# Low parts of the second MLP matrix: an accumulating DMA in place of a subtraction on DVE

## The chip, the cores and the metric

The kernel runs on one core of one Trainium2 chip. The metric is the device time of one execution in microseconds (us); lower is better. TensorE is written PE here, VectorE DVE, ScalarE ACT, GpSimd POOL and SyncE SP, as the profile writes them.

## What is computed

The reference is a decoder trunk of two layers on one sequence of 256 tokens, 1024 channels wide, all in float32. Layer 0 mixes tokens by stick-breaking attention, layer 1 by causal softmax attention with rotary positions (its block selection is void at 256 tokens, since there is one block). After each mixer comes an MLP with a squared ReLU. Cut to what matters here:

```python
def squared_relu_mlp(x, w1, w2):
    return jnp.square(jax.nn.relu(x @ w1)) @ w2
...
    for i in range(DEPTH):
        ln1_g, ln1_b, w1, w2, ln2_g, ln2_b = channel[i]
        h = layer_norm(DEEPNORM_ALPHA * h + mixers[i % N_MIXERS](h), ln1_g, ln1_b)
        h = layer_norm(DEEPNORM_ALPHA * h + squared_relu_mlp(h, w1, w2), ln2_g, ln2_b)
```

`w1` is 1024 x 4096 and `w2` is 4096 x 1024, so each of them is 16 MB per layer.

## The kernel before

**Three products for one.** PE multiplies in the type fp32r. To keep float32 accuracy, every operand is split in two fp32r numbers: `hi`, the operand rounded to fp32r, and `lo`, what the rounding left. Each dense product is then three matmuls, hi by hi, hi by lo and lo by hi (`mm3`, and the three `mm` calls in `projT`), all summed in PSUM. So every weight that comes from memory has to be split on the chip before PE can use it.

**Units.** The weights come in units of 1 MB, tiles of 128 x 4 x 512 float32: for each layer 12 units of `wqkv`, 4 of `wo`, 16 of `w1` and 16 of `w2`, in the order of the list `units`. The units are numbered through both layers, 0 to 95; layer 0 has units 0 to 47. `Unit` queues for each unit one load on SP's DMA queue into a `raw` tile (line 242), and two halves of 128 x 1024, each split by `split`: ACT copies `raw` to `hi`, which rounds (line 203), and DVE subtracts `hi` from `raw` to give `lo` (line 204). There are three `raw` buffers (`RAWS`) and five pairs of `hi` and `lo` (`LIVE`). A `raw` buffer is free again when the second half has been split, a `hi`/`lo` pair when PE has done its last matmul with the unit (`retire`).

**The MLP.** It runs in 8 steps of 512 hidden channels, numbered 0 to 7. `up_tok` (steps 0 and 1) and `up` (steps 2 to 7) multiply by two units of `w1`; ACT and DVE make the squared ReLU (lines 624 and 626), and the hidden values are split as well. `down` multiplies the hidden values of one step by two units of `w2`, first for the first 128 tokens, then for the other 128, and adds all 8 steps up in four PSUM banks. After the two first `up` steps the kernel goes on with up 2, down 0, up 3, down 1 and so on until up 7, down 5; then come down 6 and down 7 and the closing norm. So in steady state one MLP step takes four units from memory: two of `w1` and two of `w2`. In `down` the loop goes over four k with the two units in turn, so the second half of a unit is first needed at k = 2.

**The order of the work.** No scheduler of a library decides it: the class `Plan` does, while the program is built. Each operation is queued with the engine, a cost, the results it needs, the buffer slots it takes and gives back, and a rank; `Plan` keeps a clock for each engine and emits operations in the order in which they can start by these clocks, the most urgent first among those that can start within 0.25 us. PE's dense products stand in the order of the program, and small products slip in between. Once emitted, each engine takes its instructions strictly in that order and waits on semaphores for what they need.

**POOL** has little to do: it fills constants, writes one column in the scores of layer 0, adds the rotary parts in layer 1 (line 540) and takes one power for each norm (line 362).

Of the kernel before, what the change touches and what calls it, by code (L numbers as in the profile page):

```python
# [7 lines left out]
F32 = mybir.dt.float32  # L8
# [3 lines left out]
ALU = mybir.AluOpType  # L12
# [18 lines left out]
MARGIN, WINDOW = 0.5, 0.25  # L31
# [8 lines left out]


class Tok:
    """When the result of one queued operation is there, by the plan's clock (None: not yet emitted)."""

    def __init__(self, eng=None, end=None, lat=0.0):
        self.eng, self.end, self.lat = eng, end, lat
# [3 lines left out]


class Late:
    """Both halves of v, which are queued later than their readers."""

    def __init__(self):
        self.toks = []
# [4 lines left out]


class Plan:
    """Emits the operations of all engines in the order in which they can start.

    TensorE follows the dense products as the program gives them. Everything else is queued with
    its cost (us), the results it needs, the buffer slots it takes and gives back, and a rank
    (lower is more urgent), and is emitted once TensorE's clock has passed its start. Operations
    queued for TensorE itself slip in between the dense products when their operands have been
    there for MARGIN; among operations that can start within WINDOW the most urgent goes first.  # L70
    """

    LAT = {"pe": 0.2, "act": 0.1, "dve": 0.1, "pool": 0.2, "sp": 1.0}

    def __init__(self, slots):
        self.clock = {e: 0.0 for e in self.LAT}
# [77 lines left out]
def trunk(ctx: ExitStack, tc: tile.TileContext, x, xt, cst, cstb, w, ln, out):  # L154
    nc = tc.nc
# [4 lines left out]
    one = pool("one", 1)  # L160
# [9 lines left out]
    plan = Plan({"raw": RAWS, "split": LIVE, "t2k": N2K, "t1k": N1K, "pt": NPT, "kd": NKD, "st": 3, "acc": 4, "wk": 4})  # L170
    clock = plan.clock
# [10 lines left out]
    def act(n, fn, **kw):  # L182
        return plan.op("act", 0.06 + 0.00083 * n, fn, **kw)
# [14 lines left out]
        return Tok("pe", clock["pe"], 0.2)  # L198

    def split(n, hi, lo, src, after, rank=1, take=(), give=(), scale=None):  # L200
        """hi(), lo(), src() give the operands when the operation is emitted."""
        if scale is None:
            f = lambda: nc.scalar.copy(hi(), src())  # L203
            g = lambda: nc.vector.tensor_tensor(lo(), src(), hi().bitcast(F32), op=ALU.subtract)  # L204
        else:
            f = lambda: nc.scalar.mul(hi(), src(), scale)
            g = lambda: nc.vector.scalar_tensor_tensor(lo(), src(), scale, hi().bitcast(F32), op0=ALU.mult, op1=ALU.subtract)
        a = act(n, f, after=after, rank=rank, take=take)
        b = dve(n, g, after=[a], rank=rank, give=give)
        b.first = a  # L210
        return b
# [4 lines left out]
    v = [one.tile([P, D], F32, tag=f"v{t}", name=f"v{t}") for t in range(NT)]  # L216
# [13 lines left out]
    taken = [0]  # L230
    U = []

    class Unit:
        def __init__(self, i):
            name, j = units[i]
            steps = [(k, k + 1) for k in range(4)] if i < 2 else [(0, 2), (2, 4)]
            self.tok = []
            for k0, k1 in steps if i < 2 else [(0, 4)]:
                def load(k0=k0, k1=k1):
                    if k0 == 0:  # L240
                        self.raw = raws.tile([P, 4, 512], F32, tag="raw", name=f"raw{i}")
                    nc.sync.dma_start(self.raw[:, k0:k1, :], w[name][j][:, k0:k1, :])
                ld = plan.op("sp", 0.73 * (k1 - k0), load, rank=3 + 0.01 * i + 0.001 * k0, take=[("raw", 1)] if k0 == 0 else ())
                for c0, c1 in steps:
                    if not (k0 <= c0 and c1 <= k1):
                        continue

                    def hi(c0=c0, c1=c1):
                        if c0 == 0 and not hasattr(self, "hi"):
                            self.hi = splits.tile([P, 4, 512], F32R, tag="hi", name=f"hi{i}")  # L250
                            self.lo = splits.tile([P, 4, 512], F32R, tag="lo", name=f"lo{i}")
                        return self.hi[:, c0:c1, :]
                    b = split(512 * (c1 - c0), hi, lambda c0=c0, c1=c1: self.lo[:, c0:c1, :],
                              lambda c0=c0, c1=c1: self.raw[:, c0:c1, :], after=[ld] + [k.first for k in self.tok[:1]],
                              rank=lambda c0=c0: (0.5 if i < taken[0] else 1 if i < taken[0] + 1 else 2) + 0.001 * i + 0.0001 * c0,
                              take=[("split", 1)] if c0 == 0 else (), give=[("raw", 1)] if c1 == 4 else ())
                    self.tok += [b] * (c1 - c0)

    def take(n):
        i = taken[0]  # L260
# [39 lines left out]
    for k in range(KT):  # L300
        src = xs[k // 4][:, k % 4, :]
        if k in X_LOADS:
            ks = slice(k, k + X_LOADS[k])
            ld = plan.op("sp", max(0.45, 0.365 * X_LOADS[k]), lambda ks=ks: nc.sync.dma_start(
                xs[ks.start // 4][:, ks.start % 4:(ks.stop - 1) % 4 + 1, :], xt[:, ks, :]), rank=3 + 0.01 * (k // 4) + 0.001 * (k % 4) - 0.0005)
        if k == 0:
            hi = dve(T * 0.5, lambda k=k, src=src: nc.vector.tensor_copy(xh[:, k, :], src), after=[ld], rank=0.01 * k)
        else:
            hi = act(T, lambda k=k, src=src: nc.scalar.copy(xh[:, k, :], src), after=[ld], rank=0.5 + 0.00005 * k)
# [92 lines left out]
    for l in range(DEPTH):  # L402
# [2 lines left out]
        mixed = {}  # L405

        def attend(g, pr, src, ready, give):
            """Heads 4g + 2pr and the next: scores, weights, their transposes, the products with v."""
            box = {}

            def part(s, k):
                """s: high or low parts; k: of which head's keys (None: of the queries)"""
                def go():
                    if k is None:
                        box["q"] = box.get("q") or buf("q", F32R)
                        return box["q"][:, s * T:(s + 1) * T]
                    if "kd" not in box:
                        box["kd"] = kd_free.pop(0)
                    return kd[box["kd"]][s][k * HD:(k + 1) * HD, k, :]
                return go  # L420
            ks = []
            for k in (0, 1):
                ks.append(split(T, part(0, k), part(1, k), lambda k=k: src()[k * HD:(k + 1) * HD, T:2 * T],
                                after=ready + [y.first for y in ks], rank=0.9, take=[("kd", 1)] if k == 0 else ()))
            q = split(T, part(0, None), part(1, None), lambda: src()[:, 0:T], after=ready + [y.first for y in ks], rank=0.9,
                      take=[("t2k", 1, 4)], give=give, scale=SCALE)
            s1, p1 = weights(1, box, ks + [q])
            _, p0 = weights(0, box, ks + [q, s1])
            flipped = [flip(j, box, [p1, p0]) for j in range(2)]

            def mix():
                if g // 2 not in OT:
                    OT[g // 2] = (st.tile([P, 4, T], F32R, tag="sh", name="oh"), st.tile([P, 4, T], F32R, tag="sl", name="ol"))
                o = box["o"] = wbank("o")
                for kt in range(2):
                    for j in range(2):
                        hd = 4 * g + 2 * pr + j
                        pt = box["pt", j]
                        nc.tensor.matmul(o[HD * j:HD * j + HD, kt * P:T], v[kt][:, hd * HD:(hd + 1) * HD],  # L439
                                         pt[:, 0:T] if kt == 0 else pt[:, T:T + P], start=kt == 0, stop=kt == 1)  # L440
            m = plan.op("pe", 0.74, mix, after=flipped + [vtok[g // 2]], rank=0.5,
                        take=[("wk", 1)] + ([("st", 1)] if g % 2 == 0 and pr == 0 else []), give=[("pt", 2)])
            pi = 2 * (g % 2) + pr
            mixed[g, pr] = split(T, lambda: OT[g // 2][0][:, pi, :], lambda: OT[g // 2][1][:, pi, :],
                                 lambda: box["o"][:, :T], after=[m], rank=0.8, give=[("wk", 1)])

        def weights(t, box, ready):
            """Scores of two heads for query tile t (head by head along the free axis) and what becomes of them."""
            nk = (t + 1) * P
            n = 2 * nk  # L450
            tag = "t2k" if t else "t1k"

            def scores():
# [6 lines left out]
                if t == 0:  # L460
                    kd_free.append(box["kd"])
            s = plan.op("pe", 0.76 if t else 0.43, scores, after=ready, rank=1.05 - 0.05 * t, take=[("wk", 1, 1)],
                        give=() if t else [("t2k", 1), ("kd", 1)])
            sc = lambda: box["sc", t][:, :n]
            new = lambda name: (t2k if t else t1k).tile([P, 516 if t else 260], F32, tag=tag, name=name)
            if l == 0:
# [7 lines left out]
                k = act(n, sig("keep", -1.0), after=[s], rank=0.7, take=[(tag, 1, 1)])  # L474
                b = act(n, sig("p", 1.0), after=[k], rank=0.69, take=[(tag, 1)], give=[("wk", 1)])
# [312 lines left out]
```

## Time and profile before

| what | us |
|---|---|
| median of 2 runs | 617.45 |
| the two runs | 616.89 and 618.01 |
| span of the profiled execution, first to last instruction | 616.2 |
| PE busy in it | 601.4 |
| DVE busy | 400.9 |
| ACT busy | 300.3 |
| POOL busy | 26.4 |

The profiled execution is told by its span alone; the runs are timed as a whole, so the median stands 1.25 us above the span. An engine's busy time is the time in which at least one of its instructions ran. Matmuls overlap each other in the records (each is shown for longer than the distance to the next), so how fast PE really goes is read from the distance between the starts of two matmuls. A DMA is issued by an engine in a moment and runs on 16 DMA engines that all queues share; "DMA share" is the mean busy share of these 16.

### The profile page before, as it was taken

To read this page: it belongs to the slowest core of one execution; us is meant where nothing else is said; L and a number is where in the kernel's file an instruction comes from. 1 tells how busy PE (TensorE), PEld (TensorE's weight loads), DVE (VectorE), ACT (ScalarE), POOL (GpSimd) and SP (SyncE) were. 2 spreads that over 40 slices of the span, in tenths; PEclk is the share of its full clock that TensorE was granted. 3 is DMA by queue.
4 is the path that set the end of the run, shared out by engine and by line. 5 is a ranking of instruction groups with operands and counts; after the bars stand their busy time and mean duration, and the time that the engine had idled before them with its cause. 6 is when DMAs were issued, how large, how long until landed. Compare 5 with 4: busy or idle time off the path is not lost.

```text
span 616.2 us, 8736 instructions
## 1 busy us (share of the span) xinstructions
PE 601.4 (98%) x3544; PEld 515.7 (84%) x3544; DVE 400.9 (65%) x537; ACT 300.3 (49%) x483; POOL 26.4 (4%) x46
## 2 busy tenths in 40 slices
PE   8999999999999999999999999999999999999994
PEld 6888887888998898898887777778898998898883
DVE  5888776596636446455788868858676536446444
ACT  5866764245535344353436755635365335344310
POOL 2000000000000000000032011101000000000000
PEclk9999999999999999999999999999999999999998
DMA  8875235265564555546273543332874464555201
GB/s 282 348 298 215 82 128 194 76 227 217 200 246 145 202 200 187 199 160 228 71 252 132 189 153 137 138 137 70 271 260 152 169 241 152 198 198 190 84 1 68
DMA packets 17752, 109.32 MB, mean 177 GB/s; under 512 B 1968, under 2 KB 2352, under 8 KB 5680
## 3 DMA queue, kind: packets, MB, share of 16 engines
q1 hardware_dynamic: 17712, 108.76, 48.1%
q8 instruction: 28, 0.46, 0.3%
q14 instruction: 12, 0.10, 0.0%
HBM read 107.71 MB, written 1.05 MB: 176 GB/s over the span
## 4 chain that ended last, share of the span: by engine, by line
PE 87%; DVE 8%; ACT 1%; DMA 1%; issue 1%; POOL 0%; SPq 0%; DVEq 0%; ACTq 0%
PE up_ps L189 29%; PE dn_ps L189 29%; PE wo_ps L189 7%; PE qk_ps L189 5%; PE qkT_ps L189 5%; PE v_ps L189 4%; PE sc L189 2%; DVE lo L204 2%; PE o L439 2%; DVE keep L476 1%; DVE p L479 1%; DMA raw<-in_wqkv 1%; PE xt L378 1%; PE pt_ps L504 1%; PE ht_ps L658 1%
## 5 line engine op out<-in xcount | busy, mean ns | idle before, releaser
L204 DVE TENSOR_TENSOR lo<-raw,hi 128x1024 fp32r<-128x1024 f32 (+1 forms) x196 | 229.7, 1215 | 73.5 <-ACT hi L203 73.0
L203 ACT CAST hi<-raw 128x1024 fp32r<-128x1024 f32 (+1 forms) x196 | 192.2, 1034 | 91.0 <-issue 65.2
L189 PE MATMUL up_ps<-xh,hi 128*128 128x256 f32 x384 | 108.1, 281 | 0.0
L189 PE MATMUL up_ps<-xl,hi 128*128 128x256 f32 x384 | 107.9, 281 | 0.0
L189 PE MATMUL up_ps<-xh,lo 128*128 128x256 f32 x384 | 107.9, 281 | 0.0
L189 PE MATMUL dn_ps<-hi,hl 128*128 128x512 f32 x256 | 100.8, 394 | 0.0
L189 PE MATMUL dn_ps<-lo,hh 128*128 128x512 f32 x256 | 100.2, 392 | 0.0
L189 PE MATMUL dn_ps<-hi,hh 128*128 128x512 f32 x256 | 99.6, 389 | 0.0
L189 PEld LDWEIGHTS up_ps<-xl,hi 128*128 128x128 f32 x384 | 72.3, 188 | 0.5
L189 PEld LDWEIGHTS up_ps<-xh,hi 128*128 128x128 f32 x384 | 72.3, 188 | 0.5
L189 PEld LDWEIGHTS up_ps<-xh,lo 128*128 128x128 f32 x384 | 72.4, 188 | 0.0
L626 DVE SCALAR_TENSOR_TENSOR r<-up_ps,r 128x512 f32<-128x512 f32 x32 | 22.1, 691 | 59.9 <-ACT r L624 59.9
L624 ACT ACTIVATE r<-up_ps 128x512 f32<-128x512 f32 x32 | 19.2, 599 | 77.9 <-PE up_ps L189 77.9
L189 PEld LDWEIGHTS dn_ps<-lo,hh 128*128 128x128 f32 x256 | 48.0, 188 | 10.6
L189 PEld LDWEIGHTS dn_ps<-hi,hh 128*128 128x128 f32 x256 | 48.1, 188 | 10.1
L189 PEld LDWEIGHTS dn_ps<-hi,hl 128*128 128x128 f32 x256 | 48.1, 188 | 9.8
L189 PE MATMUL qkT_ps<-xh,hi 128*128 128x256 f32 x128 | 37.7, 295 | 1.3 <-ACT hi L203 1.3
L189 PE MATMUL qkT_ps<-xh,lo 128*128 128x256 f32 x128 | 36.4, 285 | 0.2 <-DVE lo L204 0.2
L189 PE MATMUL qkT_ps<-xl,hi 128*128 128x256 f32 x128 | 36.3, 283 | 0.0
L203 ACT CAST xh<-xt 128x512 fp32r<-128x512 f32 x12 | 6.7, 589 | 42.9 <-PE xt L378 42.9
L189 PE MATMUL v_ps<-hi,xh 128*128 128x512 f32 x64 | 27.3, 427 | 0.0
L189 PEld LDWEIGHTS qkT_ps<-xh,hi 128*128 128x128 f32 x128 | 24.6, 192 | 2.8 <-ACT hi L203 2.4
(114 smaller groups left out, 922.5 us busy)
## 6 DMA issues: line engine op xcount, KB each, us to landing
raw<-in_w SPq DMA_DIRECT2D x64, 1024.0 KB, 4.8
raw<-in_wqkv SPq DMA_DIRECT2D x22, 1024.0 KB, 5.2
raw<-in_wo SPq DMA_DIRECT2D x8, 1024.0 KB, 4.8
raw<-in_wqkv SPq DMA_DIRECT2D x8, 256.0 KB, 6.3
gb<-in_l_ln_g SPq DMA_DIRECT2D x4, 512.0 KB, 3.8
gb<-in_l_ln_b SPq DMA_DIRECT2D x4, 512.0 KB, 5.3
h<-in_x SPq DMA_DIRECT2D x2, 512.0 KB, 6.1
out<-h SPq DMA_DIRECT2D x4, 256.0 KB, 2.1
```

The source lines that it names most:

```text
L189: nc.tensor.matmul(ps, sta, mov, start=start, stop=stop)
L203: f = lambda: nc.scalar.copy(hi(), src())
L204: g = lambda: nc.vector.tensor_tensor(lo(), src(), hi().bitcast(F32), op=ALU.subtract)
L378: nc.tensor.transpose(ps[:, k * P:(k + 1) * P], h[t][:, (4 * n + k) * P:(4 * n + k + 1) * P], ident)
L439: nc.tensor.matmul(o[HD * j:HD * j + HD, kt * P:T], v[kt][:, hd * HD:(hd + 1) * HD], pt[:, 0:T] if kt == 0 else pt[:, T:T + P], start=kt = ...
L476: c = dve(n, lambda: nc.vector.tensor_tensor_scan(box["keep", t][:, 0:n][:, ::-1], box["keep", t][:, 0:n][:, ::-1], ind[n][:, ::-1], 1.0, ...
L479: return s, dve(n, lambda: nc.vector.tensor_tensor(box["p", t][:, :n], box["p", t][:, :n], box["keep", t][:, 1:n + 1], op=ALU.mult), after ...
L504: nc.tensor.transpose(ps[:, 0:P], p0[:, j * P:(j + 1) * P], ident)
L624: nc.scalar.activation(box["r", n], ps, AF.Relu)
L626: return dve(512, lambda: nc.vector.scalar_tensor_tensor(box["r", n], ps, 0.0, box["r", n], op0=ALU.max, op1=ALU.mult), after=[a], rank=0. ...
L658: nc.tensor.transpose(box["ht"][:, k * P:(k + 1) * P], box["r", 0][:, k * P:(k + 1) * P], ident)
```

## The change

For the units of `w2` of steps 0 to 5 (`j < 12`, 12 of 16 units in each layer, 24 in all) the low part is made in another way. ACT makes `hi` as before. Then ACT writes minus `raw` into the `lo` tile, which rounds it, so that the tile holds minus `hi`. Then POOL issues a DMA that adds `raw` to what stands in the `lo` tile, and leaves raw minus hi there. The DVE subtraction of these units is gone. `raw` is given back when the DMA's second half is done, by the plan's clock of a new queue `gd` with a cost of 0.0016 us per column and a latency of 2.5 us. The comments that the full diff takes out change nothing and are left out here; the lines below line 61 move down by some 20 lines.

```diff
-    LAT = {"pe": 0.2, "act": 0.1, "dve": 0.1, "pool": 0.2, "sp": 1.0}
+    LAT = {"pe": 0.2, "act": 0.1, "dve": 0.1, "pool": 0.2, "sp": 1.0, "gd": 2.5}
...
+                    if by_dma(name, j):
+                        b = self.split_dma(i, c0, c1, hi, ld)
+                        self.tok += [b] * (c1 - c0)
+                        continue
                     b = split(512 * (c1 - c0), hi, lambda c0=c0, c1=c1: self.lo[:, c0:c1, :],
...
+        def split_dma(self, i, c0, c1, hi, ld):
+
+            n = 512 * (c1 - c0)
+            rank = lambda: (0.5 if i < taken[0] else 1 if i < taken[0] + 1 else 2) + 0.001 * i + 0.0001 * c0
+            raw = lambda: self.raw[:, c0:c1, :]
+            lo = lambda: self.lo[:, c0:c1, :]
+            a = act(n, lambda: nc.scalar.copy(hi(), raw()), after=[ld] + [k.first for k in self.tok[:1]], rank=rank,
+                    take=[("split", 1)] if c0 == 0 else ())
+            m = act(n, lambda: nc.scalar.mul(lo(), raw(), -1.0), after=[a], rank=rank)
+            b = plan.op("gd", 0.0016 * n, lambda: nc.gpsimd.dma_start(lo().bitcast(F32), raw(), accum_op=ALU.add), after=[m], rank=rank,
+                        give=[("raw", 1)] if c1 == 4 else ())
+            b.first = m
+            return b
+
+    def by_dma(name, j):
+        return name[:2] == "w2" and j < 12
```

Since `Plan` sets the order of every engine, the change moves instructions. The first place is ACT in a step in the middle of the first MLP, from the squared ReLU of up 4 to that of up 5; units 33 and 36 are of `w1`, 34 and 35 of `w2`, and `up_ps`, `r`, `hh` are the hidden values of the `up` step. Before:

```order
L624 ACTIVATE r_2062<-up_ps_1939 128x512
L203 CAST hi33_2067<-raw33_1933 128x1024
L203 CAST hh_2055<-r_2062 128x512
L203 CAST hi33_2067<-raw33_1933 128x1024
L203 CAST hi34_2084<-raw34_2000 128x1024 x2
L203 CAST hi35_2133<-raw35_2029 128x1024 x2
L203 CAST hi36_2156<-raw36_2106 128x1024 x2
L624 ACTIVATE r_2242<-up_ps_2128 128x512
```

And with the change:

```order
L203 CAST hi33_2079<-raw33_1946 128x1024
L203 CAST hh_2065<-r_2074 128x512
L203 CAST hi33_2079<-raw33_1946 128x1024
L269 CAST hi34_2096<-raw34_2033 128x1024
L271 ACTIVATE lo34_2097<-raw34_2033 128x1024
L269 CAST hi34_2096<-raw34_2033 128x1024
L271 ACTIVATE lo34_2097<-raw34_2033 128x1024
L269 CAST hi35_2147<-raw35_2069 128x1024
L271 ACTIVATE lo35_2148<-raw35_2069 128x1024
L269 CAST hi35_2147<-raw35_2069 128x1024
L271 ACTIVATE lo35_2148<-raw35_2069 128x1024
L203 CAST hi36_2187<-raw36_2119 128x1024 x2
```

Each half of units 34 and 35 now has two instructions on ACT, the copy and the negated copy, one right behind the other; the units keep their order.

On POOL nothing stood between the power of the first norm of a layer and that of its closing norm; now the layer's 24 DMAs stand there, two for each of its 12 units, in the order in which ACT feeds them.

The second place is SP's queue of weight loads in the same steps, with the semaphores that each load waits for. `DVE_49` stands for a DVE instruction, `DMAHW` for an earlier load, `DMASW` for one of POOL's DMAs. Before:

```order
L242 DMA raw37_2123<-in_w10 128x2048 [waits DMAHW5_49,DVE_49]
L242 DMA raw38_2190<-in_w20 128x2048 [waits DMAHW6_49,DVE_49]
L242 DMA raw39_2219<-in_w20 128x2048 [waits DMAHW7_49,DVE_49]
L242 DMA raw40_2296<-in_w10 128x2048 [waits DMAHW0_49,DVE_49]
L242 DMA raw41_2313<-in_w10 128x2048 [waits DMAHW1_49,DVE_49]
```

And with the change:

```order
L242 DMA raw37_2140<-in_w10 128x2048 [waits DMASW5_49,DMAHW5_49,DMASW4_49,Activation_49]
L242 DMA raw38_2227<-in_w20 128x2048 [waits DMAHW7_49,DVE_49]
L242 DMA raw39_2263<-in_w20 128x2048 [waits DMAHW6_49,DMASW7_49,DMASW6_49]
L242 DMA raw40_2313<-in_w10 128x2048 [waits DMAHW0_49,DVE_49]
L242 DMA raw41_2334<-in_w10 128x2048 [waits DMASW1_49,DMAHW1_49,DMASW0_49,Activation_49]
```

The loads stand in the same order. Every second one now waits for two of POOL's DMAs, those of the unit of `w2` whose `raw` buffer it takes over (raw37 that of unit 34, raw39 that of unit 35, raw41 that of unit 38). On PE the dense products keep their order; in each MLP the four small transposes of the second `up_tok` for the second 128 tokens (line 658, `ht_ps`) stand one product of three matmuls earlier.

## Rows read from the trace of the kernel before

**Rows 1.** The page: span; busy time and share of each engine.

```profile
span 616.2 us, 8736 instructions
...
PE 601.4 (98%) x3544; PEld 515.7 (84%) x3544; DVE 400.9 (65%) x537; ACT 300.3 (49%) x483; POOL 26.4 (4%) x46
```

**Rows 2.** Stretches: columns named in the first row.

```profile
core 0: us, PE busy (x) PEld busy (x) DVE busy (x) ACT busy (x) POOL busy (x), PEclk, DMA share, GB/s
...
11.00:28.00 17.00, 16.88 (x112) 15.05 (x113) 14.27 (x23) 14.08 (x29) 0.00 (x0) 1.00 0.90 355
28.00:103.00 75.00, 71.90 (x519) 62.11 (x519) 56.30 (x75) 48.87 (x91) 0.77 (x11) 1.00 0.52 191
103.00:308.00 205.00, 205.00 (x1197) 180.42 (x1194) 125.61 (x145) 91.49 (x114) 2.98 (x3) 1.00 0.49 182
...
404.00:606.00 202.00, 202.00 (x1182) 177.80 (x1179) 118.03 (x137) 82.79 (x103) 2.77 (x3) 1.00 0.45 164
606.00:616.20 10.20, 1.94 (x9) 1.26 (x7) 5.04 (x9) 0.00 (x0) 0.92 (x1) 0.75 0.14 51
```

**Rows 3.** Stretches: one MLP step, columns as in rows 2.

```profile
195.30:217.70 22.40, 22.40 (x146) 20.39 (x146) 11.94 (x12) 10.07 (x13) 0.00 (x0) 1.00 0.50 189
```

**Rows 4.** Groups by line: count, busy us, mean ns, idle before.

```profile
L204 DVE TENSOR_TENSOR lo<-raw,hi 128x1024 fp32r<-128x1024 f32 x188 | 224.2, 1237 | 71.7 <-ACT hi L203 71.2
L203 ACT CAST hi<-raw 128x1024 fp32r<-128x1024 f32 x188 | 187.2, 1052 | 88.0 <-issue 65.2 <-PE qk_ps L189 11.8 <-DMA raw<-in_wqkv 5.1
...
L624 ACT ACTIVATE r<-up_ps 128x512 f32<-128x512 f32 x32 | 19.2, 599 | 77.9 <-PE up_ps L189 77.9
```

**Rows 5.** Timeline of ACT there: start, duration, instruction, idle time before.

```profile
208.86 2.95 ACT L203 CAST hi<-raw 128x1024 fp32r<-128x1024 f32 x3
217.25 3.89 ACT L203 CAST hi<-raw 128x1024 fp32r<-128x1024 f32 x4 [5.45 <-issue]
226.42 0.60 ACT L624 ACTIVATE r<-up_ps 128x512 f32<-128x512 f32 x1 [5.27 <-PE up_ps L189]
...
229.75 1.04 ACT L203 CAST hi<-raw 128x1024 fp32r<-128x1024 f32 x1
```

**Rows 6.** Timeline of DVE in that step.

```profile
218.33 4.63 DVE L204 TENSOR_TENSOR lo<-raw,hi 128x1024 fp32r<-128x1024 f32 x4 [4.63 <-ACT hi L203]
...
230.82 1.22 DVE L204 TENSOR_TENSOR lo<-raw,hi 128x1024 fp32r<-128x1024 f32 x1 [0.25 <-ACT hi L203]
```

**Rows 7.** Timeline of PE there: down ends, later the next begins.

```profile
217.23 0.39 PE L189 MATMUL dn_ps<-lo,hh 128*128 128x512 f32 x1
217.46 0.39 PE L189 MATMUL dn_ps<-hi,hl 128*128 128x512 f32 x1
...
229.28 0.39 PE L189 MATMUL dn_ps<-lo,hh 128*128 128x512 f32 x1
...
229.97 0.39 PE L189 MATMUL dn_ps<-lo,hh 128*128 128x512 f32 x1
...
232.71 0.39 PE L189 MATMUL dn_ps<-lo,hh 128*128 128x512 f32 x1
```

**Rows 8.** Timeline, start of the first MLP: ACT, then PE.

```profile
150.41 0.60 ACT L624 ACTIVATE r<-up_ps 128x512 f32<-128x512 f32 x1 [1.18 <-PE up_ps L189]
...
153.69 0.59 ACT L203 CAST hh<-ht_ps 128x512 fp32r<-128x512 f32 x1 [0.79 <-PE ht_ps L658]
...
162.93 0.39 PE L189 MATMUL dn_ps<-lo,hh 128*128 128x512 f32 x1
```

**Rows 9.** The page: DMA issues, KB each, median us to landing.

```profile
raw<-in_w SPq DMA_DIRECT2D x64, 1024.0 KB, 4.8
...
gb<-in_l_ln_g SPq DMA_DIRECT2D x4, 512.0 KB, 3.8
...
h<-in_x SPq DMA_DIRECT2D x2, 512.0 KB, 6.1
```

**Rows 10.** Line 242, the weight loads: time from issue to landing.

```profile
DMA to landing us min/median/max: 3.0/4.9/9.5
```

## The prediction

> **What bounds the kernel now.** I read the page first, then the kernel cut into stretches, then one MLP step in the timelines. The page says that PE is busy for 601.4 of 616.2 us [rows 1]. The stretches say where the rest lies: from 103 to 308 us and from 404 to 606 us, which hold both MLPs, PE is busy for 205.00 of 205.00 and 202.00 of 202.00 us; the last 10.2 us lack 8.3, the first attention lacks 3.1 [rows 2]. All that the change touches lies in the two stretches without a gap. Busy time alone does not tell that PE goes at its full pace, so I compare distances: with DVE idle two matmuls of a down step start 0.23 us apart (217.23 to 217.46; DVE had been idle for 4.63 us up to 218.33), and with DVE at work 12 of them take 2.74 us (229.97 to 232.71), again 0.23 each [rows 6, 7]. DVE's work does not slow PE, and in an MLP step DVE is busy for 11.94 of 22.4 us, ACT for 10.07, POOL for nothing, the DMA engines for half the time [rows 3]. So PE bounds the MLP, and what is taken from DVE there is taken from an engine that nobody waits for. The question is only whether the new way is late.
>
> **The change, part by part.**
>
> DVE loses 48 subtractions of 1.237 us [rows 4], 59.4 us; in a step 4 of them, so that 11.94 falls to 7.0 us. PE never waits there: worth 0.
>
> ACT gains 48 negated copies. The trace has no such instruction; half its size takes 0.60 us, the plain copy of its size 1.05 [rows 4], so between 1.05 and twice 0.60. I take 1.05: 50 us in all, 4.2 in a step, so 10.07 becomes 14.3 of 22.4. They fit: the copies that began at 208.86 ended at 211.8 and are now done at 213.9, before the next that PE lets go at 217.25; these ended at 221.1, now 223.2, and the squared ReLU that waits behind them came at 226.42 [rows 5]. Worth 0; its cover is 3.2 us, and what is over that would delay hidden values that PE needs over a step later.
>
> POOL gains 48 DMA issues where it did nothing [rows 3]. Behind them on POOL stands only the power of the closing norm, after two more down steps on PE.
>
> Now the wait that takes DVE's place: PE waits for the accumulating DMA. Call A its time from issue to landing. ACT begins unit 35 at 217.25, when PE has let a hi/lo pair go; copy and negated copy of its first half are done 2 x 1.05 later, at 219.35, and PE first reads this low part at 229.97 (the second lo matmul of the step; the first, at 229.28, is unit 34's) [rows 5, 7]. So A may be 10.6 us. The second half is issued at 221.45 and read 12 matmuls later, at 232.71: 11.3 us. Unit 34 is made a down step earlier, from about 209.9 on, and has over 17. The tightest is unit 23, in the first down step of each layer: ACT's ReLU ends at 151.0, three instructions of 1.05 (the last negated copy of unit 22, copy and negated copy of unit 23) stand before the DMA, which is issued at 154.2, and PE reads at 162.93 [rows 8]: 8.8 us.
>
> No DMA of POOL and none that accumulates is in this trace, so A is bounded by the loads: the fastest took 3.0 us, the slowest 9.5 [rows 10]; 512 KB, the size of one half, took 3.8 in one kind and 6.1 in another [rows 9]. I take 4.8, between the last two and what 1 MB takes. Then 4.0 us are spare at unit 23 and 5.8 at unit 35 and its like, and the wait is worth 0. At 9.5, unit 23 comes 0.7 us late, once per layer: +1.4 us. At 3.0 nothing is won, because PE has no gap there to lose.
>
> The `raw` buffer is held until the second DMA has landed, so every second load starts later. Unit 37's load waits for unit 34's second half, which ACT feeds at 213.9: landing at 218.7, the load then lands 4.8 later, at 223.5, and ACT copies unit 37 from 229.75 on [rows 5, 9]. 6.2 us are spare (A up to 11.0). Unit 39's load waits for unit 35: 221.45 + 4.8 + 4.8 = 231.1, and its copy comes a step after 217.25, at 239.6. Worth 0. The loads behind them on SP's queue move with them and have as much.
>
> The DMA engines take on 24 MB more. In a step four loads keep them at 0.50 of 22.4 us [rows 3], 11.2 us, 2.8 for each MB. One accumulating DMA takes 1.4 us of them by the bytes that it writes, 2.8 if its two streams are read one after the other, 4.2 if reading both and writing all add up. I take 2.0, nearer to what 512 KB take now. Four of them make 8.0, together 19.2 of 22.4, a share of 0.86; the engines did 0.90 from 11 to 28 us [rows 2]. Worth 0, with little to spare.
>
> On this price a page of the Trainium skill speaks against the change. "Collectives: The Full Stack", in its section on the bandwidth ceiling, says that an add in the DMA engines costs nothing for the adding, but half the speed, since two sources are read through one ring. By that rule the price is the 2.8 of above and the sum is that of the first rival below; no run here shows it yet.
>
> Last, four transposes in each MLP come three matmuls (0.36 us) earlier on PE; ACT's part of their operand ended at 151.0 and DVE's behind it takes under 1 us, while the copy that waited for them began at 153.69 [rows 8]. Worth 0.
>
> The sum is 0: the span stays 616.2 us, and with the 1.25 us by which the median of the runs stands above it the kernel takes 617.45, so 617.5. By the bounds of A and of the negated copy alone it is 617.4 to 619. A measurement can tell about 2% from no change, 12.3 us.
>
> **The rivals.**
>
> *The DMA engines become the bound.* At 2.8 us a step needs 11.2 + 11.2 = 22.4 us of them. If they do no better than the 0.90 of the fullest stretch [rows 2], a step takes 24.9, 2.5 more. There are six such steps in a layer, 15.0 us; the 5.8 us that unit 35 has to spare are used up first; 9.2 are left, 18.4 in both layers: 636. It passes 12.3 us from 2.7 us per DMA on. At 4.2 a step takes 31.1, and both layers lose 93: 710. For it speaks that the loads alone fill half the time; against it, that a copy of this size now takes half as much.
>
> *The DMA is slow to land.* POOL may need long to issue, or the second half waits behind the first. Since ACT starts unit 35 only when PE gives a pair back, every us of A above 10.6 is lost anew in each step. With A at 12.2, twice the 6.1 us of the slower 512 KB load [rows 9], five units lose 1.6 and unit 23 loses 3.4: 11.4 per layer, 22.8 in both: 640. It passes 12.3 us from A = 11.3 on. Against it: the slowest of all loads, of twice the size, took 9.5 [rows 10].
>
> *PE gains after all.* Then it has to be in its gaps: 14.8 us in all, less the 8.3 at the end that the norm holds [rows 2], leaves 6.5: 611. For it speaks only that DVE is at 65% [rows 1]. Over 2% faster would need nearly all gaps of the kernel.
>
> That the subtraction stays where it was is not open: the instructions are gone from DVE's queue.
>
> **How the numbers follow.** The forecast has 0.70, engines full 0.13, slow landing 0.12, a gain 0.05. Of the two slow cases (0.25) about 0.03 stay under 12.3 us; of the gain 0.02 would have to come from somewhere I don't see. So faster 0.02, same 0.70 + 0.03 + 0.03 = 0.76, slower 0.22. The forecast's own range is 616 to 619. The whole one goes down to 614, half of the possible gain, and up to 640, the price of slow landing, past the 636 of two reads; the three-pass price and slower landings stay outside, about 0.12.
>
> **What would show it.** Right: PE still busy all through both MLPs, DVE busy down by about 59 us and ACT's up by about 50, POOL's DMAs landing within 3 to 9 us, DMA share in a step near 0.86, and the step still 22.4 us from one unit of that kind to the next. Engines full: a share of 0.9 or more through the steps, loads that take 8 us and more, ACT waiting for `raw` and PE for `lo` or `hi` late in each MLP, steps that grow. Slow landing: a wait of PE for the DMA once in every step, always at the second triple of the down step, with a share well below 0.9. The forecast is wrong if PE has any gap of over 1 us in the steps.

## The result, and the profile after

| what | before | after |
|---|---|---|
| median of 2 runs, us | 617.45 | 626.73 (625.18 and 628.29) |
| ratio | | 1.0133, 95% interval 1.0088 to 1.0178 |
| span of the profiled execution, us | 616.2 | 623.4 |

The kernel is 1.3% slower. That is within 2%, as forecast, and inside the whole range of 614 to 640, but outside the forecast's own range of 616 to 619 and 9.2 us above its 617.5. The first experiment below, a longer series of the same kernel, agrees. The profiled execution is the one of 625.18 us, and its span is 7.2 us longer than before; this 7.2 is what the traces can explain.

Line numbers up to 252 are the same in both kernels, those further down are 21 higher with the change (624 becomes 645); L269, L271 and L272 are the copy, the negated copy and the DMA of `split_dma`. The page of after, against [rows 1, 9]; the lines with `q` give packets, MB and the share of all 16 DMA engines over the span:

```profile
span 623.4 us, 8882 instructions
...
PE 603.8 (97%) x3544; PEld 515.0 (83%) x3544; DVE 346.6 (56%) x489; ACT 347.1 (56%) x531; POOL 68.6 (11%) x94
...
q1 hardware_dynamic: 17712, 108.76, 47.3%
q0 software_dynamic: 6912, 25.17, 21.2%
...
raw<-in_w SPq DMA_DIRECT2D x64, 1024.0 KB, 6.9
lo<-raw POOLq DMA_DIRECT2D x48, 512.0 KB, 8.4
```

DVE fell by 54.3 us and ACT rose by 46.8, much as forecast. `q0` is POOL's queue: its 48 DMAs take 21.2% of 623.4 us, 132 us, 2.75 us of all 16 engines each. They land 8.4 us after their issue, and a weight load now takes 6.9 us instead of 4.8.

The stretches of after, against [rows 2, 3]:

```profile
103.00:308.00 205.00, 203.25 (x1186) 177.82 (x1183) 95.81 (x117) 112.27 (x135) 24.08 (x27) 1.00 0.80 241
404.00:606.00 202.00, 198.25 (x1174) 172.96 (x1173) 88.44 (x106) 108.89 (x131) 22.61 (x26) 1.00 0.76 224
150.00:174.50 24.50, 23.26 (x151) 20.88 (x150) 8.78 (x10) 16.52 (x21) 4.50 (x6) 1.00 0.95 278
195.30:217.70 22.40, 22.40 (x146) 20.41 (x145) 7.40 (x8) 13.60 (x17) 3.17 (x5) 1.00 0.96 278
219.20:242.20 23.00, 22.59 (x145) 20.19 (x144) 7.40 (x8) 13.03 (x16) 3.29 (x4) 1.00 0.95 270
```

PE, gapless in both long stretches before, now lacks 1.75 and 3.75 us there. The loss is not spread over the steps: one step (195.30 to 217.70) is as gapless as before and another (219.20 to 242.20) lacks 0.41 us, while the DMA engines are at 0.95 or 0.96 in the three short stretches; in the step from 195.30 to 217.70 they were at 0.50 before. The granted clock of PE is 1.00 in all these stretches, so it has no part in this.

Who waited for a DMA in after (us in total, times, longest):

```profile
ACT hi L203 <- DMA raw<-in_w: 63.9, 14, 7.2
...
PEld dn_ps L189 <- DMA lo<-raw: 9.1, 10, 2.2
...
PE dn_ps L189 <- DMA lo<-raw: 5.4, 6, 1.8
```

And SP's queue of weight loads:

```profile
SPq L242 <- DMA lo<-raw: 179.8, 24, 11.6
```

24 loads now stand until an accumulating DMA has given back their `raw` buffer. That a load waits is not new: in the trace of before SP's queue stood for 468.6 us until DVE's subtractions had given buffers back.

Every wait that PE has in the two long stretches is for the accumulating DMA. Its longest, in the second MLP, in the timeline of PE, with the wait in brackets:

```profile
579.98 0.39 PE L189 MATMUL dn_ps<-hi,hh 128*128 128x512 f32 x1
582.18 0.50 PE L189 MATMUL dn_ps<-lo,hh 128*128 128x512 f32 x1 [1.81 <-DMA lo<-raw]
582.52 0.40 PE L189 MATMUL dn_ps<-hi,hl 128*128 128x512 f32 x1
```

The place is the second low-part matmul of a down step, unit 91's, the kind that [rows 7] priced. From 579.98 to 582.18 it is 2.20 us instead of 0.23, and the next distance is 0.34: 2.08 lost where the bracket shows 1.81. If each of the six waits hides the same 0.27 (an estimate from this one), 5.4 becomes 7.0 of the 7.2 us. So nearly the whole loss of this execution is PE waiting for `lo`. Four of the six waits are for the second half of the step's second unit, two, as here, for its first half.

How a DMA comes to be late, here the second half of the same unit 91, is in the chain of waits of after, cut to 554 to 586 us (start, duration, what):

```profile
554.54 9.18 DMA raw<-in_w
...
563.80 1.05 ACT hi L203
...
573.02 0.96 ACT lo L271
573.99 0.34 issue
574.33 11.61 DMA lo<-raw
...
585.98 4.17 PE dn_ps L189 x17
```

And ACT's row for the copy in it, in the timeline:

```profile
563.80 1.05 ACT L203 CAST hi<-raw 128x1024 fp32r<-128x1024 f32 x1 [6.08 <-DMA raw<-in_w]
```

Read from the top. At 554.54 a weight load starts, that of unit 89, as soon as unit 86's `raw` buffer, which an accumulating DMA had held, is free. It needs 9.18 us. ACT stands idle in front of its copy for 6.08 of them, with units 90 and 91 queued behind it, so the second DMA of unit 91 is issued only at 574.33. It takes 11.61 us, and PE waits for it until 585.98. A late accumulate makes a load late, and a late load makes the next accumulate late: a loop through three `raw` buffers. This one chain shows the loop; the run with four buffers below tests it.

### The profile page after: what moved, and what is told of

Its sections match the earlier page's. It is cut to its first block, busy times and chain, and to the rows that moved or that the text cites. A ratio compares the mean times of both kernels' runs of the same rounds, so it can differ in the third digit from the quotient of the medians.

```text
span 623.4 us, 8882 instructions
## 1 busy us (share of the span) xinstructions
PE 603.8 (97%) x3544; PEld 515.0 (83%) x3544; DVE 346.6 (56%) x489; ACT 347.1 (56%) x531; POOL 68.6 (11%) x94
## 3 DMA queue, kind: packets, MB, share of 16 engines
q0 software_dynamic: 6912, 25.17, 21.2%
HBM read 107.71 MB, written 1.05 MB: 174 GB/s over the span
## 4 chain that ended last, share of the span: by engine, by line
PE 59%; DMA 20%; DVE 7%; ACT 6%; issue 5%; POOL 1%; SPq 0%; DVEq 0%; POOLq 0%; ACTq 0%
PE dn_ps L189 17%; PE up_ps L189 14%; DMA lo<-raw 11%; PE wo_ps L189 7%; DMA raw<-in_w 7%; PE qk_ps L189 5%; PE qkT_ps L189 4%; PE v_ps L189 4%; DVE lo L204 3%; DMA raw<-in_wqkv 3%; PE sc L189 2%; PE o L460 2%; ACT hi L203 2%; POOL lo L272 1%; ACT lo L271 1%
## 5 line engine op out<-in xcount | busy, mean ns | idle before, releaser
L204 DVE TENSOR_TENSOR lo<-raw,hi 128x1024 fp32r<-128x1024 f32 (+1 forms) x148 | 175.0, 1214 | 157.8 <-ACT hi L203 150.2
L203 ACT CAST hi<-raw 128x1024 fp32r<-128x1024 f32 (+1 forms) x148 | 146.3, 1029 | 89.9 <-DMA raw<-in_w 63.9
L272 POOL DMA_DIRECT2D lo<-raw x48 | 41.9, 872 | 243.1 <-ACT lo L271 177.7
L189 PEld LDWEIGHTS dn_ps<-lo,hh 128*128 128x128 f32 x256 | 48.1, 188 | 18.8 <-DMA lo<-raw 9.1
L189 PEld LDWEIGHTS dn_ps<-hi,hh 128*128 128x128 f32 x256 | 48.1, 188 | 10.1
L189 PEld LDWEIGHTS dn_ps<-hi,hl 128*128 128x128 f32 x256 | 48.1, 188 | 10.0
L271 ACT ACTIVATE lo<-raw 128x1024 fp32r<-128x1024 f32 x48 | 50.7, 1055 | 0.0
L269 ACT CAST hi<-raw 128x1024 fp32r<-128x1024 f32 x48 | 49.9, 1039 | 1.1 <-DMA raw<-in_w 0.8
```

Source lines behind the costliest of these rows:

```text
L189: nc.tensor.matmul(ps, sta, mov, start=start, stop=stop)
L269: a = act(n, lambda: nc.scalar.copy(hi(), raw()), after=[ld] + [k.first for k in self.tok[:1]], rank=rank, take=[("split", 1)] if c0 == 0 ...
L271: m = act(n, lambda: nc.scalar.mul(lo(), raw(), -1.0), after=[a], rank=rank)
L272: b = plan.op("gd", 0.0016 * n, lambda: nc.gpsimd.dma_start(lo().bitcast(F32), raw(), accum_op=ALU.add), after=[m], rank=rank, give=[("raw ...
```

## The experiments

Each run stands against runs of the kernel before on the same chip; ratios with 95% intervals decide, since the median of before itself was 618.2 to 618.8 in the three series. The theory after the result: the accumulating DMAs, which read two sources, fill the DMA engines in the steps, and then the lead that the prediction worked out is used up. The rivals: ACT's extra copies; the longer wait itself, whatever the DMA does; the loop through the held `raw` buffers.

**The change once more,** with more executions, no edit.

> The changed kernel once more, to have its time from more runs and beside the others of this set. Engines full: 6 to 10 us slower than before; the gaps of PE in the steps add up to the difference of the spans and all stand at a dn_ps<-lo matmul, that is at a wait for POOL's DMA. Held raw buffers: PE's gaps would stand at up_ps or at hi as well.

Measured: 625.14 us, ratio 1.0104 (1.0073 to 1.0136). Its waits:

```profile
ACT hi L203 <- DMA raw<-in_w: 66.1, 16, 6.8
...
PE dn_ps L189 <- DMA lo<-raw: 6.2, 7, 1.5
```

PE waits for the same DMA seven times, where it was six. The waits stand in part at the same places as in the first profile (in both at 490, 494 and 586 us and, much shorter here, at unit 23's second half near 166 us), in part in other steps (here at 186, 191 and 563 us, there at 235 and 582): some steps are late in both executions, but not always the same ones.

**The instructions alone.** ACT's negated copy stays, and DVE's subtraction writes over it; no DMA of POOL.

```diff
-            b = plan.op("gd", 0.0016 * n, lambda: nc.gpsimd.dma_start(lo().bitcast(F32), raw(), accum_op=ALU.add), after=[m], rank=rank,
+            b = dve(n, lambda: nc.vector.tensor_tensor(lo(), raw(), hi().bitcast(F32), op=ALU.subtract), after=[m], rank=rank,
```

> ACT writes the negated copies as with the change, but DVE then overwrites them with its subtraction as before, and POOL issues no DMA. It tells what ACT's 50 us alone cost. Engines full and slow landing both expect no change, 617 to 618.5 us and PE without a gap in the steps. If ACT's added work were part of the loss, some of the 7 to 9 us would show here.

Measured: 1.0014 (0.9998 to 1.0029). A step of it:

```profile
195.30:217.70 22.40, 22.40 (x146) 20.42 (x145) 12.21 (x12) 13.81 (x16) 0.00 (x0) 1.00 0.51 190
```

ACT is as busy as in the changed kernel (13.81 us in a step, against 13.60) and PE has no gap. The work on ACT by itself costs at most the 0.3% to which the interval reaches, and no gap of PE shows any of it.

**A plain copy in place of the accumulate.** Same issue, same waits, same bytes written, one source read. (`lo` then holds `raw`: the kernel leaves out the subtraction, and the products with `lo` take `raw` in place of the low part.)

```diff
-            b = plan.op("gd", 0.0016 * n, lambda: nc.gpsimd.dma_start(lo().bitcast(F32), raw(), accum_op=ALU.add), after=[m], rank=rank,
+            b = plan.op("gd", 0.0016 * n, lambda: nc.gpsimd.dma_start(lo().bitcast(F32), raw()), after=[m], rank=rank,
```

> The same DMAs, but they copy raw over lo instead of adding to it (lo holds raw; everything else, the order included, is as with the change). Engines full by the two reads: the engines' time for one falls from about 2.75 us to about 1.4, the share in a step from 0.97 to about 0.75, landing from 8.4 to about 5, and the time to 617 to 619 us. Slow landing: landing stays at 8 us and the time at 625. If the copy costs the engines as much as the add, the two reads are not what fills them.

Measured: 0.9991 (0.9979 to 1.0002). Its page and one step:

```profile
q0 software_dynamic: 6912, 25.17, 10.4%
...
raw<-in_w SPq DMA_DIRECT2D x64, 1024.0 KB, 6.2
lo<-raw POOLq DMA_DIRECT2D x48, 512.0 KB, 6.2
```

```profile
195.30:217.70 22.40, 22.40 (x146) 20.43 (x145) 7.40 (x8) 13.86 (x17) 2.15 (x4) 1.00 0.84 286
```

And its loads' wait for the copies:

```profile
SPq L242 <- DMA lo<-raw: 137.4, 24, 10.1
```

With the same packets and bytes `q0` takes half the share: 10.4% of 615.6 us, 1.33 us each. The DMAs land in 6.2 us, and the loss is gone, although 24 loads still wait for POOL's DMAs, 137.4 us in all. So neither the longer way of `lo` nor the held `raw` buffer costs anything by itself; what costs is the accumulate, at twice the price of a copy. That the second read makes it twice, and not the adding, is argued from what the DMA has to fetch; no run separates the two. The share in the step (0.84) and the landing (6.2 us) came out above the 0.75 and 5 that were expected: beside the copies the loads' own queue `q1` took 50.3% of the engines, against 48.1% before.

**Half and three quarters of the DMAs.** First only the second unit of each pair, 24 DMAs:

```diff
-        return name[:2] == "w2" and j < 12
+        return name[:2] == "w2" and j < 12 and j % 2 == 1
```

> Only the second w2 unit of each of the steps 0 to 5 is made by the DMA (12 units, 24 DMAs instead of 48); these are the ones with the short lead (8.8 and 10.6 us). Engines full: the DMA share in a step falls to about (11.2 + 2 x 2.7) / 22.4 = 0.74, the DMAs land in about 5 us, PE never waits for one, and the time goes back to 617 to 619 us. Slow landing (a DMA of POOL takes 8 to 10 us by itself): landing stays at 8 us or more, unit 23 is still late, and the time stays above 620. Held raw buffers: ACT still waits for loads, about half as long as with the full change.

Then three of four units (`j % 4 != 0` in the same place), 36 DMAs:

> 36 DMAs instead of 48 (the second unit of every step 0 to 5 and the first of steps 1, 3 and 5). Engines full: the share in the steps is about (11.2 + 3 x 2.7) / 22.4 = 0.86, landing between the 5.6 us of 24 DMAs and the 8.4 of 48, PE waits for a DMA at most once or twice, 617.5 to 621 us. If the loss grew with the number of DMAs alone, it would be three quarters of 7 to 9 us: 623 to 625.

Measured: 24 DMAs 1.0003 (0.9988 to 1.0019), 36 DMAs 1.0000 (0.9989 to 1.0012). The stretch from 150 to 285 us, first with 24, then with 36, columns as in [rows 2]:

```profile
150.00:285.00 135.00, 135.00 (x872) 123.04 (x871) 62.30 (x66) 73.51 (x88) 10.61 (x12) 1.00 0.77 244
```

```profile
150.00:285.00 135.00, 135.00 (x871) 123.05 (x870) 55.26 (x59) 79.20 (x93) 15.85 (x18) 1.00 0.90 266
```

And with all 48:

```profile
150.00:285.00 135.00, 133.25 (x860) 120.48 (x859) 45.09 (x50) 82.61 (x97) 20.61 (x24) 1.00 0.97 277
```

ACT's wait for `raw` before line 203, with 24 and with 36:

```profile
ACT hi L203 <- DMA raw<-in_w: 3.0, 2, 2.5
```

```profile
ACT hi L203 <- DMA raw<-in_w: 12.2, 8, 2.7
```

The share goes from 0.77 to 0.90, and to 0.97 with all 48; the loss comes only with the other twelve, the first units of steps 0, 2 and 4. It is not in proportion to the number of DMAs: with 36 of them no loss is seen (0.1% either way), twelve more cost 6 to 9 us. PE waited once in the profile with 36, for 0.5 us. ACT's wait for `raw` goes 3.0, 12.2, 63.9: with 24 it is far less than the half of 63.9 that a price of the held buffers alone would give.

**The traffic alone.** The kernel before, its subtractions on DVE, with 48 accumulating DMAs beside it that add a constant to a tile that nobody needs in the MLP; PE and the loads do not wait for them, and no `raw` buffer is held. They share two tiles, so POOL itself waits before it issues the next into the same tile, 192.0 us in all: at most two are under way at once, where the change can have four.

```diff
+                    if name[:2] == "w2" and j < 12:
+                        def ghost():
+                            nc.gpsimd.dma_start(v[ghosts[0] % 2], const[:, 0:D], accum_op=ALU.add)
+                            ghosts[0] += 1
+                        plan.op("gd", 0.0016 * 512 * (c1 - c0), ghost, after=[b.first], rank=3)
```

> The kernel before, with 48 accumulating DMAs of the same size added beside it, at the places where ACT has made a half of these units; they add a constant tile to v, which nobody needs in the MLP, and nobody waits for them. So the traffic is that of the change, but neither PE nor the raw buffers wait for it. Engines full: share in a step about 0.95 or more, loads land in 7 to 10 us instead of 4.8, but since the leads of 9 to 17 us are only shortened by that, the time is 617 to 620 us: the loss needs the wait for lo. If the loss came from late loads alone (or from traffic that slows PE), it would be 622 us or more here as well.

Measured: 621.93 us, 1.0058 (1.0039 to 1.0077), more than I had expected. Its waits, then ACT at the start of the first MLP (L631, L633 and L665 are lines 624, 626 and 658 of the kernel before):

```profile
ACT hi L203 <- DMA raw<-in_w: 29.3, 14, 3.0
...
PE ht_ps L665 <- DVE r L633: 2.8, 2, 1.5
```

```profile
149.54 1.05 ACT L203 CAST hi<-raw 128x1024 fp32r<-128x1024 f32 x1 [2.36 <-DMA raw<-in_w]
...
151.92 0.59 ACT L631 ACTIVATE r<-up_ps 128x512 f32<-128x512 f32 x1
```

Full engines hurt even where nobody waits for the DMA: a late load stops ACT, which works in order, and the squared ReLU behind it comes late. PE waits for its result twice, at the second `up_tok` of each layer, 2.8 us in all, of the 3.0 us by which this profile's span, 619.2 us, is longer than that of before. In no other step does PE wait. So traffic alone costs something, but in another place. What full engines alone do to a wait for `lo` this run can't tell, since PE does not read these tiles; the run with four `raw` buffers tells more.

**The price by itself.** In place of the decoder, on an otherwise idle chip: POOL's DMAs of 512 KB one after the other and eight at once, accumulating and plain, six 1 MB loads alone, and the loads with eight accumulates.

```python
    for y in many:
        nc.gpsimd.dma_start(y, src, accum_op=ALU.add)
...
    for y in cmany:
        nc.gpsimd.dma_start(y, src)
```

> Nothing of the decoder is left; the output is a constant tile. Eight accumulating DMAs of 512 KB one after the other into one tile, eight into eight tiles, the same with plain copies, six loads of 1 MB alone, six loads with eight accumulating DMAs beside them. Engines full by two reads: one accumulating DMA alone lands in 4 to 5.5 us, eight at once take the engines for about 8 x 2.7 = 22 us against 8 x 1.4 = 11 for the copies, and beside the loads both take about as long as the sum, 6 x 2.8 + 22 = 38 us. Slow landing: one alone takes 7 us or more. The time of this kernel says nothing beside the kernel before.

Measured, in a single execution: time from issue to landing, then the stretches of eight accumulates, eight copies, six loads, and loads with accumulates (columns: us, DVE, POOL, clock, DMA share, GB/s).

```profile
alone<-src POOLq DMA_DIRECT2D x8, 512.0 KB, 4.5
...
calone<-src POOLq DMA_DIRECT2D x8, 512.0 KB, 2.8
```

```profile
42.36:65.78 23.42, 0.00 (x0) 7.09 (x8) 1.00 0.95 179
93.53:106.00 12.47, 0.00 (x1) 4.16 (x8) 1.00 0.87 336
107.79:125.10 17.31, 1.20 (x11) 0.00 (x0) 1.00 0.89 363
125.49:164.16 38.67, 0.36 (x5) 7.07 (x8) 1.00 0.98 271
```

Eight accumulates keep the engines busy for 0.95 x 23.42 us, 2.8 each; eight copies for 0.87 x 12.47, 1.36 each. Loads and accumulates together take 38.67 us, nearly the 17.31 and 23.42 of the two apart (40.7): the time on the engines adds up. A single accumulate on idle engines lands in 4.5 us; the other 3.9 of the 8.4 us in the kernel come with the traffic beside it.

**Is it the held raw buffer?** The change with four `raw` buffers instead of three. For the room, two other pools are smaller, and two controls go with it: the kernel before in the same pools, and the change with three `raw` buffers in the smaller pools.

```diff
-RAWS, LIVE = 3, 5
-N2K, N1K, NPT, NKD = 10, 4, 8, 2
+RAWS, LIVE = 4, 5
+N2K, N1K, NPT, NKD = 9, 4, 5, 2
```

> The change with four raw buffers instead of three; to make room, t2k has 9 buffers instead of 10 and pts 5 instead of 8, which touches the attention alone, so the steps of the MLP are what is compared. Held raw buffers: loads start earlier, ACT no longer waits 64 us for them, PE's waits for the DMA go and the time is 617 to 620 us. Engines full: the share stays at 0.95 or more and landing at 8 us or more, PE still waits for lo, the time stays above 622.

> Before, with the subtraction on DVE, in the pools of the run with four raw buffers (one buffer more for raw, one fewer for the 2 KB tiles, three fewer for the 4 KB ones). Theory (the fourth raw buffer removes the loss of the change, and what that run still lost is the price of the smaller pools): the two attentions take some 123.5 and 120.4 us as in that run, the kernel 622 to 626, and PE still has no wait for a DMA in the steps. Rival (what it lost is the full DMA engines in another guise): the smaller pools cost nothing, attentions 121 and 119, the kernel 617.5 to 619.5.

> The change with three raw buffers, in the smaller pools alone. Theory: both losses add up: PE waits for the accumulating DMA some seven times again, 6 to 9 us in all, and the attentions take longer as in the run with four raw buffers: 629 to 633. Rival (the smaller pools cost nothing): like the change, 624 to 627, with its seven waits.

| kernel | ratio to before | 95% interval |
|---|---|---|
| change, 4 raw, smaller pools | 1.0117 | 1.0101 to 1.0133 |
| before, 4 raw, smaller pools | 1.0094 | 1.0067 to 1.0120 |
| change, 3 raw, smaller pools | 1.0179 | 1.0136 to 1.0222 |

The change with four `raw` buffers, waits:

```profile
ACT hi L269 <- DMA raw<-in_w: 4.1, 3, 2.3
...
PE dn_ps L189 <- DMA lo<-raw: 0.8, 1, 0.8
```

The change with three, in the same smaller pools:

```profile
ACT hi L203 <- DMA raw<-in_w: 66.8, 15, 6.2
...
PE dn_ps L189 <- DMA lo<-raw: 1.5, 1, 1.5
```

With the first of the three alone PE's waits were nearly gone and the time was not. The controls explain it: the smaller pools cost 0.94% with the subtraction on DVE too. Against that control the change costs 1.79 - 0.94 = 0.85% with three `raw` buffers, near the 1.04% of the old pools, and 0.23% with four, where the two intervals overlap; the intervals of the two changed kernels do not. (The first run is of another series than the two controls, and the kernel before with three `raw` buffers in the smaller pools was not run. The profile of the third kernel is of an execution of 626.4 us, the fastest of its four; PE waits once for the DMA in it, 1.5 us, where seven waits were expected.) ACT's wait for `raw` falls from 66.8 to 4.1 us, although the engines are as full as ever (from 150 to 285 us their share is 1.00):

```profile
150.00:285.00 135.00, 134.17 (x862) 121.10 (x861) 49.18 (x54) 85.41 (x101) 21.10 (x24) 1.00 1.00 282
```

What the loop does is seen in POOL's issues. The second DMA of unit 34 and the first of unit 35, in the change and then with four `raw` buffers:

```profile
219.53 0.87 POOL L272 DMA_DIRECT2D lo<-raw  x1 [1.03 <-ACT lo L271]
221.56 0.87 POOL L272 DMA_DIRECT2D lo<-raw  x1 [1.17 <-ACT lo L271]
```

```profile
217.78 0.87 POOL L272 DMA_DIRECT2D lo<-raw  x1 [1.02 <-ACT lo L271]
223.68 0.87 POOL L272 DMA_DIRECT2D lo<-raw  x1 [5.02 <-ACT lo L271]
```

With three buffers ACT comes to the first unit late, so the four DMAs of a step go out one right behind the other, 5.7 us from first to last (median of ten steps, the first of each layer left out); with four buffers the two units stand 9.5 us apart, first issue to last. From these traces, for the same ten steps, the medians of the lead (issue to PE's first read) and of the time to landing:

| DMA of the step | change: lead, landing | 4 raw: lead, landing |
|---|---|---|
| first unit, first half | 12.3, 7.5 | 17.3, 8.4 |
| first unit, second half | 13.6, 8.1 | 18.2, 9.0 |
| second unit, first half | 9.6, 9.0 | 10.4, 5.8 |
| second unit, second half | 10.8, 10.2 | 11.3, 8.7 |

The change with three buffers in the smaller pools is like the change (leads of 12.4, 13.3, 9.3 and 10.2 us), so it is the buffer and not the pools. The median landing of all 48 is 8.4 us in both columns. The loop takes lead, and at the second unit, where the lead is short, the landing is longer too: its DMAs go out close behind those of the first.

So most of the loss needs both: full engines, and the loop through three `raw` buffers. One buffer more breaks the loop, a plain copy in place of the accumulate relieves the engines, and either takes nearly all of the loss away. A buffer more is of no use here, as its room costs more than it saves. No version tried beats the kernel before. That was to be expected from [rows 2]: PE had no gap in the MLPs to lose.

## Why the prediction was right, and where it was not

*PE has nothing to gain from DVE.* Right: with DVE's 48 subtractions gone PE got nothing back, and with 36 DMAs, or with copies, the time is that of before to 0.1%.

*DVE and ACT.* Right in worth, and nearly in size. The negated copy took 1.055 us (taken: 1.05); in a step ACT was busy for 13.60 us (14.3) and DVE for 7.40 (7.0). Over the kernel DVE lost 54.3 us and not 59.4: instructions that follow each other overlap a little in the records, so that count times duration overstates busy time (in [rows 4] 188 times 1.237 is 232.6, and the busy time 224.2).

*The price on the DMA engines.* This is the step that failed. I took 2.0 us per DMA, by the bytes written with something on top; it measured 2.75 in the kernel and 2.8 alone. Four in a step make 11.0, with the loads' 11.2 that is 22.2 of 22.4 us, and the share was 0.96 instead of 0.86. The rule of the Trainium skill that I weighed and set aside, in "Collectives: The Full Stack", the section on the bandwidth ceiling, would have given 2.8. It is stated there for collectives among cores; here the trace agrees in the price, 2.75, and in the factor of two against the plain copy at 1.33.

*A, issue to landing.* Taken as 4.8 us, which is close to what it is on idle engines (4.5). In the changed kernel it was 6.2 to 11.6, with a median of 8.4:

```profile
DMA to landing us min/median/max: 6.2/8.4/11.6
```

The leads were worked out well: with the plain copy or four `raw` buffers they are 8.8 us at unit 23 and 10.4, 11.3 and 17 at unit 35, its second half and unit 34, close to the forecast. In the change the landing times reach up to them, so some steps come late and others do not. The first half of unit 23, which I took for the tightest, was not late; its second half, whose lead I had not worked out (9.2 us with the plain copy), was, in the first MLP. The two terms were not independent, as my sum had them: the load on the engines sets A.

*The held raw buffer.* Costed at nothing, with 6.2 us spare. That holds for a load of 4.8 us behind an A of 4.8. With 7.3 us for unit 86's second DMA and 9.18 for the load behind it, that of unit 89 landed at 563.7, 6.1 us after ACT stood ready for it, and the next DMA's lead shrank before its own landing grew. I had treated lead and landing as two separate budgets; they share one loop, and the leads of the first units fell by it from 17 to about 12 us.

*The rivals.* "The engines become the bound" named the right engine, and most of its signs came: share over 0.9, ACT waiting for `raw`, PE for `lo`; the loads took 6.9 us, where 8 and more was named. But its sum was not what happened. It let every step grow, at the 0.90 of the start of the kernel; at the 0.96 that was measured, 22.2 us of work need 23.1 us, some 4.4 us more in six steps, less than the 5.8 to spare, and nothing would be lost. The 7 us come from single DMAs that the loop makes late. "Slow to land" would have been late at the same triple in every step with free engines: it was not. "PE gains" is out by the plain copy, whose ratio is 0.9991 (0.9979 at the least) with less work on DVE.

So the class came out as forecast only because a loss of 1.3% is less than 2%, and the whole range held because it took in the prices of the rivals. That is luck: the mechanism, that nothing comes late, was wrong, the forecast's own range of 616 to 619 was missed, and the case that came, a slow one under 12.3 us, had a chance of about 0.03. The sign that I named as proving the forecast wrong, gaps of over 1 us in the steps, is there (2.20 us at 579.98).

## What to carry to other kernels

Price a DMA by the time it takes on the shared engines, reads and all: one that accumulates reads two sources, and here it cost twice a copy of its size (2.75 against 1.33 us for 512 KB). When the sum nears the whole step, take landing times from a full stretch and not from a quiet one, and follow each buffer that the transfer holds round to the next load: the lead can be lost on that loop while the median landing time stays the same (8.4 us here with three `raw` buffers and with four). Here the loss was a threshold: with three quarters of the DMAs none was seen, with all of them the whole of it.

## What I had not expected

Smaller pools slow PE without any wait in the trace. In the control (kernel before, four `raw` buffers, smaller pools) PE is busy without a gap in the MLP, as before, but goes more slowly through a down step:

```profile
232.40 0.39 PE L189 MATMUL dn_ps<-lo,hh 128*128 128x512 f32 x1
...
235.20 0.39 PE L189 MATMUL dn_ps<-lo,hh 128*128 128x512 f32 x1
```

These 12 matmuls take 2.80 us, against 2.74 in [rows 7], at the same granted clock of 1.00 in the MLP. Over the 768 matmuls of `down` that is 3.8 us (an estimate from these 12) of the 7.0 us between the two profiles' spans, 623.2 and 616.2. Another part may go with the granted clock, which averaged 0.90 from 11 to 28 us there, against 1.00 in [rows 2]. Other pool sizes can put the tiles at other addresses; whether that is the cause wasn't tried. And POOL is busy for 0.87 us with each issue of an accumulating DMA in the changed kernel (7.09 us for eight in the run on the idle chip), against 0.52 for a copy (4.16 for eight): small here, where POOL is idle, but a price where it is not.
